# Two parts of the RWKV-7 time mixing reordered: triangle inverses by halves, and output products that wait for a run of like matmuls

## The chip, the cores and the metric

The kernel runs on one core of a Trainium2 chip. The metric is the device time of one execution in microseconds (us). The engines are named as the profile names them: PE is TensorE (matmuls), PEld its weight loads, DVE is VectorE, ACT is ScalarE, POOL is GpSimd, SP is SyncE, whose queue issues all DMAs here.

## The reference, cut to what matters

Two layers of a streaming encoder step. Each layer projects the normalised input, runs three groups of heads on the columns (a short convolution, a latent attention, and RWKV-7 time mixing), and projects their joined output back. The change is in the time mixing alone, which is this recurrence over 1104 tokens (64 of a running stream, 16 meta tokens, 1024 of a new stream) for 4 heads of width 64:

```python
def step(s, inp):
    r_t, w_t, k_t, v_t, kk_t, a_t = inp
    sa = jnp.einsum('bhvk,bhk->bhv', s, -kk_t)
    s = (s * w_t[:, :, None, :] + sa[..., None] * (kk_t * a_t)[:, :, None, :]
         + v_t[..., None] * k_t[:, :, None, :])
    return s, jnp.einsum('bhvk,bhk->bhv', s, r_t)
```

The kernel computes it in chunks of 64 tokens: inside a chunk the steps become products of 64 by 64 matrices and the inverse of a unit triangular matrix, and only the state goes from chunk to chunk.

## The kernel before, in words

A layer has three stretches. `inproj` and `inproj_rest` run the input projections: 24 matmuls of 128x384 (or 128x336) for each block of columns and each of three groups of tokens, in fp32r, an operand split into a high and a low half (`prj<-hhi,whi` and its two companions). Attention with half of the output projection follows, and then the rest of the output projection. PE is full of projections in the first stretch, and the time mixing is slipped in between them.

The time mixing of a layer has six parts, one for each pair of heads and group of six chunks (three groups for the first pair, then three for the second). Three generators work on them. `rwkv_prep` prepares a part. `rwkv_scan` carries the state through its six chunks (`xp` reads the state, `sp` writes the next one) and ends with the output products `yp`. `rwkv_finish` normalises them (DVE, ACT), transposes them on PE (`ym`) and gates them (POOL). A generator yields the tiles and PSUM pools it needs next. `pump`, called after each matmul, asks a model of the engines (`Meter`, with an assumed cost for each instruction) when these are ready, and runs a generator whose need is due; so the program's order is fixed when the kernel is built, by that model's times. The build then places the instructions of each engine, and each engine takes its own in order.

What `rwkv_prep` does, in the order of the steps that matter here:

- It loads the columns `lora` (a buffer of which there is one), passes their first half through three ACT steps (`sigmoid`) and one DVE step, and uses it in `ldp` and `icl`.
- `chunks(X1, ...)` makes the 64 by 64 matrices of the part, in 24 matmuls whose operands are 64 rows by 64 columns (`x<-wb,wx 64*64`).
- Their 16 by 16 diagonal blocks are summed out by DVE (`dg<-wq`), written to DRAM and read back with one block in each of 48 partitions (`tri`): two transfers in a row. There DVE inverts the 48 unit triangles in a loop over `n = 1 .. 14`, two instructions a step, a multiply into the scratch half `tm` and an add. A copy makes the transpose, and three transfers (one out, two in: `dg`, `dt`) bring both back, spread out by `wq<-dg,cst` and `wa<-dt,cst`.
- From the blocks' inverses the 64 by 64 inverses are put together by `inv` products, first 24 with `chunks(X2, ...)` (24 more `x`) behind them, then 48, then 24 with 48 `av` and `yv` products, then 24, and after these 48 `w`. All are matmuls of the 64*64 form.

A stretch of PE's order in which only such 64*64 matmuls stand is called a run here. `yp` is of the same form: 24 matmuls. In the kernel before, `rwkv_scan` issues them as soon as the state's last step is there (`yield uv, "rs"`). `prep` of part i+1 starts when the scan of part i has begun, and `scan` of part i+1 when its preparation is made, so a scan runs beside the next part's preparation.

Of the kernel before, what the change touches and what calls it, by code (L numbers as in the profile page):

```python
# [15 lines left out]
ALU = mybir.AluOpType  # L16
AX = mybir.AxisListType
# [14 lines left out]
GN = 384  # L32
# [4 lines left out]
BLK = 16  # L37
# [157 lines left out]
class Net:  # L195
# [729 lines left out]
    def rwkv_prep(self, l, i, g, hp):  # L925


        nc, I, O = self.nc, self.I, self.O
        tag = self.rwkv_tag(i)
        S = lambda s: self.S(tag, s)  # L930
        gc = slice(GN * g, GN * (g + 1))
        lora = self.small("lora", [128, 512])[:, :GN]
        nc.sync.dma_start(lora, self.zd[6, :, gc])
        wl = lora[0:64]
        self.sigmoid(wl, wl, 2.0)
# [2 lines left out]
        r, k, v = (wr[:, GN * x:GN * (x + 1)] for x in range(3))  # L938
# [23 lines left out]
        for t in range(3):  # L962
# [3 lines left out]
                                in0=ps[:, :GN].rearrange("p (t f) -> p t f", f=128),  # L966
                                in1=self.w0b[:, hc].unsqueeze(1).to_broadcast([128, 3, 128]), op=ALU.add)
# [16 lines left out]
        for t in range(3):  # L984
            tri = self.c(C_TRI0 if g == 0 and t == 0 else C_TRI, 128)
# [38 lines left out]
        def chunks(X, lhs, m, swap):  # L1024
            pj = [rp("x0"), rp("x1")]
            for t, c in quad:
                x = 1 - c if swap else c
                for j in range(2):
                    self.mm(pj[j][cr(x), 128 * t:128 * (t + 1)].rearrange("p (i n) -> p i n", i=2), lhs[cr(j), t, c, :],
                            arc(t, c, j), start=True, stop=True)  # L1030

            def masked(j):
                p3 = pj[j][:, :GN].rearrange("p (t n) -> p t n", t=3)
                nc.vector.tensor_tensor(out=X[:, j], in0=p3, in1=msk(m, 128), op=ALU.mult)
                if X is X1:
                    nc.scalar.activation(A[:, j], p3[:, :, 0:64], AF.Copy)
            return masked

        masked = chunks(X1, bk, C_X1, True)
        for j in range(2):  # L1040
            masked(j)
# [3 lines left out]
                                op=ALU.add, axis=AX.X)  # L1045
        scr = nc.dram_tensor(f"tri{l}_{g}_{hp}", (3, 6, 8, BLK, BLK), F32).ap()
        nc.sync.dma_start(scr[0].rearrange("t b r k -> (b r) t k"), dg)
        tri = self.small("tri", [128, 512])[:48].rearrange("p (i r k) -> p i r k", i=2, k=BLK)
        nc.sync.dma_start(tri[:, 0], scr[0].rearrange("t b r k -> (t b) r k"))
        yield kt, "rw"  # L1050
        for ts in ((0, 1, 2), (3, 4, 5)):
            o = turned(lambda t: wx[:, 128 * t:128 * (t + 1)], ts)
# [10 lines left out]
        o = turned(lambda t: v[:, 128 * t:128 * (t + 1)])  # L1063
# [2 lines left out]
        nc.scalar.activation(at, turned(lambda t: wb[:, GN * t:GN * t + 128]), AF.Copy)  # L1066

        up, tm = tri[:, 0], tri[:, 1]
        for n in range(1, BLK - 1):
            o = [48, n, BLK - 1 - n]  # L1070
            nc.vector.tensor_tensor(out=tm[:, :n, n + 1:], in0=up[:, :n, n:n + 1].to_broadcast(o), in1=up[:, n:n + 1, n + 1:].to_broadcast(o),
                            op=ALU.mult)
            nc.vector.tensor_tensor(out=up[:, :n, n + 1:], in0=up[:, :n, n + 1:], in1=tm[:, :n, n + 1:], op=ALU.add)
        nc.gpsimd.memset(tri[:, 0].rearrange("p r k -> p (r k)")[:, 0:BLK * BLK:BLK + 1], 1.0)
        nc.vector.tensor_copy(tm, up.rearrange("p r k -> p k r"))
        nc.sync.dma_start(scr[1:3].rearrange("x t b r k -> (t b) x r k"), tri)
        dq, dt = dg, self.small("dt", [128, 6, BLK])
# [10 lines left out]
        def prod(lhs, rhs, ps, cc=slice(0, 64)):  # L1088
            o = ps[:, :GN].rearrange("p (t n) -> p t n", n=64)
            for t in range(6):  # L1090
                for c in range(2):
                    self.mm(o[cr(c), t, cc], lhs[cr(c), t, :], rhs[cr(c), t, cc], start=True, stop=True)
            return o

        def block(dst, r, cc, o):
            rows = lambda c: slice(64 * c + r.start, 64 * c + r.stop)
            nc.scalar.activation(dst[rows(0), :, cc], o[rows(0), :, cc], AF.Copy)
            nc.vector.tensor_copy(dst[rows(1), :, cc], o[rows(1), :, cc])

        mk = lambda i: self.lev[:, i].unsqueeze(1).to_broadcast([128, 6, 64])  # L1100
        yield Q, Tm, kt, "rw+", "next"
        o = prod(A, Tm, self.psp("inv"))
        masked = chunks(X2, kt, C_X2, False)
        nc.scalar.activation(Pm, o, AF.Copy)
        yield Pm, "rw+"
        oq, ot = prod(Pm, Q, rp("inv")), prod(Q, Pm, rp("inv"))
        nc.vector.copy_predicated(Q, mk(0), oq)
        nc.vector.copy_predicated(Tm, mk(1), ot)
# [2 lines left out]

        lo, hi = slice(0, 32), slice(32, 64)
        yield Q, Tm, X2, uv, "rw+", "next"
        inv = prod(A, Tm, self.psp("inv"), lo)
        ps = [rp("av"), rp("yv")]
        o = [x[:, :GN].rearrange("p (j t n) -> p j t n", j=2, n=64) for x in ps]
# [6 lines left out]
        self.evict(AV, o[0])  # L1123
        self.evict(X2[:, :, :, 64:128], o[1])
        yield Pm, Q, "rw"
        block(Q, lo, hi, prod(Pm, Q, rp("inv"), hi))
        yield Q, AV, at, "rw+"

        ps = [rp("w"), rp("w")]
        o = lambda c, j, x: ps[c][cr(j), 192 * x:192 * (x + 1)].rearrange("p (t n) -> p t n", n=64)  # L1130
# [12 lines left out]
    def rwkv_scan(self, l, i, g, hp, dc, wb, kb, uv, wq, wx):  # L1143

        nc, I, O = self.nc, self.I, self.O
        rp = lambda s: self.ps(s, "rs")
        v4 = lambda x, n: x.rearrange("p (j t n) -> p j t n", j=2, n=n)
        X1, X2, QAV = v4(wq[:, 0:768], 128), v4(wx[:, 0:768], 128), v4(wq[:, 768:1152], 64)
        quad = [(t, c) for t in range(3) for c in range(2)]
        cr = lambda c: slice(64 * c, 64 * c + 64)  # L1150
        two = lambda x: x.rearrange("p (j n) -> p j n", j=2)
        if g == 0:
            nc.gpsimd.memset(X2[cr(1), :, 0, 0:64], 0.0)
        for t, c in quad:
            ci = 2 * t + c
            sample, meta = g == 0 and ci == 0, g == 0 and ci == 1
            b = cr(1 - c)
            if sample:
                s = self.state_tile()
                for j in range(2):  # L1160
                    nc.sync.dma_start(s[cr(j), cr(j)], I["wkv"][l, hp, cr(j), :])
            elif not meta:
                s = self.state
            if meta:
                nc.vector.tensor_copy(two(uv[b, ci, :]), QAV[b, :, t, :])
            else:
                yield s, "rs"
                sd = self.small("sd", [128, 128])
                nc.scalar.activation(sd, s, AF.Copy, scale=dc[:, ci:ci + 1])
                ps = rp("xp")  # L1170
                self.mm(ps[:, 0:128], wb[:, GN * t + 128 + 128 * c:GN * t + 256 + 128 * c], s, start=True, stop=True)
                nc.vector.tensor_tensor(out=two(uv[b, ci, :]), in0=two(ps[b, 0:128]), in1=QAV[b, :, t, :], op=ALU.add)
                nc.scalar.activation(X2[cr(c), :, t, 0:64], two(ps[cr(c), 0:128]), AF.Copy)
            yield uv[b, ci, :], "rs"
            ps = rp("sp")
            self.mm(ps[:, 0:128], kb[:, ci, :], uv[:, ci, :], start=True, stop=True)
            last = g == 2 and ci == 5
            dst = self.state_tile()
            for j in range(2):
                b = cr(j)  # L1180
                if meta:
                    nc.vector.tensor_scalar(dst[b, b], ps[b, b], dc[b, ci:ci + 1], None, op0=ALU.mult)
                else:
                    nc.vector.scalar_tensor_tensor(out=dst[b, b], in0=ps[b, b], scalar=dc[b, ci:ci + 1], in1=sd[b, b],
                                                   op0=ALU.mult, op1=ALU.add)
            if sample or last:
                for j in range(2):
                    nc.sync.dma_start(O["wkv"][l, 1 if sample else 0, hp, cr(j), :], dst[cr(j), cr(j)])
            self.state = dst
        nc.gpsimd.tensor_tensor(out=X2[:, :, :, 0:64], in0=X2[:, :, :, 0:64], in1=X2[:, :, :, 64:128], op=ALU.add)  # L1190
        yield uv, "rs"

        ps = rp("yp")
        for t in range(3):
            for j in range(2):
                for c in range(2):
                    b = cr(1 - c)
                    self.mm(ps[cr(c), 128 * t + 64 * j:128 * t + 64 * j + 64], X1[b, j, t, 64:128], uv[b, 2 * t + c, cr(j)],
                            start=True, stop=True)
        self.scanned = ps, wq, wx  # L1200
# [32 lines left out]
    def mix(self, main, side, streams, fill):  # L1233

        self.solo = self.prepped = self.projected = self.valued = self.queried = self.halved = False
        self.scored = self.steps = self.spent = 0
        streams = [[(), q] for q in streams]
        early = streams[ORDER.index("prepare")]
        self.side = [[(), q] for q in side] + [early]
        for _ in main:  # L1240
            pass
        self.projected, self.spent = True, NEVER
        self.side.remove(early)
        self.race(streams, fill)
        assert not self.side
# [292 lines left out]
```

## Time and profile before

| | |
|---|---|
| time, three runs | 1533.61, 1536.56 and 1537.31 us; median 1536.56 us |
| the profiled execution | 1536.26 us; span from the first to the last instruction 1534.3 us |
| PE, PEld | 1459.0 us busy (95%), 1306.4 us (85%) |
| DVE, ACT, POOL | 1063.0 us (69%), 769.3 us (50%), 258.0 us (17%) |
| granted TensorE clock | 0.989 of full speed, mean over the span |

PE's share says that only some 75 us of the span had no matmul in flight. These are spread over many waits of a few us or less, so the waits of PE, and what stands ahead of them on the other engines, are what to read. [...]

### The profile page before, as it was taken

The page shows a single profiled execution, that of the slowest core. Times are in us where ns is not written, and L with a number is a line of the kernel's source. Part 1 is how long each engine was busy: PE and PEld are TensorE (multiplying, and loading weights), DVE is VectorE, ACT ScalarE, POOL GpSimd, SP SyncE. Part 2 cuts the span into 40 slices and gives each one's busy share as a digit, 9 for nine tenths or more (in the row PEclk, how much of TensorE's full clock was granted, in tenths as well). Part 3 has the DMA queues.
Part 4 walks back from the last instruction along what each step waited for, and adds up shares of the span by engine and source line. Part 5 has one row for each costly group of instructions (what it writes and reads, how often), then busy time and mean ns, then how long its engine had stood idle before and what let it go on. Part 6 is the DMA issues. An engine that isn't in the chain of part 4 may idle for free.

```text
span 1534.3 us, 30679 instructions
## 1 busy us (share of the span) xinstructions
PE 1459.0 (95%) x12060; PEld 1306.4 (85%) x12060; DVE 1063.0 (69%) x2623; ACT 769.3 (50%) x1842; POOL 258.0 (17%) x281
## 2 busy tenths in 40 slices
PE   7999998999999999999999998899999999999996
PEld 7989887988887878779999888788988888778796
DVE  7566586766869676585845575876867787577666
ACT  7125454343668575563522354444456775555442
POOL 0212212221221101000011221312112211011002
PEclk9999999999999999999999999999999999999998
DMA  6332112322325101122423312122212341002123
GB/s 220 124 90 91 54 42 65 87 40 64 99 69 174 44 25 40 57 70 63 150 93 104 111 38 57 55 61 78 62 56 80 106 141 47 28 22 85 47 66 118
DMA packets 95327, 119.82 MB, mean 78 GB/s; under 512 B 41872, under 2 KB 74768, under 8 KB 95184
## 3 DMA queue, kind: packets, MB, share of 16 engines
q1 hardware_dynamic: 95184, 117.87, 25.0%
q8 instruction: 95, 1.56, 0.4%
q14 instruction: 48, 0.39, 0.1%
HBM read 81.24 MB, written 36.60 MB: 77 GB/s over the span
## 4 chain that ended last, share of the span: by engine, by line
PE 65%; DVE 17%; ACT 8%; issue 5%; DMA 3%; POOL 2%; SPq 0%; DVEq 0%; ACTq 0%; POOLq 0%
PE prj L81 33%; PE sc L81 6%; PE po L81 6%; PE tr L81 5%; DVE tri L81 3%; PE upq L81 3%; PE inv L81 3%; DVE wq L81 2%; PE val L81 1%; ACT wq L81 1%; DVE wlo L81 1%; DVE st L81 1%; PE upk L81 1%; PE tm L81 1%; PE w L81 1%
## 5 line engine op out<-in xcount | busy, mean ns | idle before, releaser
L81 PE MATMUL prj<-hhi,whi 128*128 128x384 f32 (+1 forms) x1152 | 391.3, 340 | 7.3 <-ACT hhi L81 6.4
L81 PE MATMUL prj<-hlo,whi 128*128 128x384 f32 (+1 forms) x1152 | 390.7, 339 | 0.6 <-DVE hlo L81 0.6
L81 PE MATMUL prj<-hhi,wlo 128*128 128x384 f32 (+1 forms) x1152 | 390.0, 339 | 0.8 <-DVE wlo L81 0.8
L81 PEld LDWEIGHTS prj<-hhi,whi 128*128 128x128 f32 x1152 | 218.6, 190 | 10.8 <-ACT hhi L81 6.4
L81 PEld LDWEIGHTS prj<-hlo,whi 128*128 128x128 f32 x1152 | 218.5, 190 | 4.9 <-DVE hlo L81 1.0
L81 PEld LDWEIGHTS prj<-hhi,wlo 128*128 128x128 f32 x1152 | 218.5, 190 | 3.8 <-DVE wlo L81 1.1
L81 PE MATMUL prj<-yhi,wo 128*128 128x384 f32 (+2 forms) x776 | 208.5, 338 | 2.1 <-DVE xn L81 2.0
L81 PE MATMUL sc<-ka,qa 128*128 128x264 f32 (+8 forms) x720 | 154.6, 335 | 3.9 <-ACT p L81 3.1
L81 ACT ACTIVATE p<-sc,st 128x144 f32<-128x144 f32 (+8 forms) x240 | 128.1, 542 | 42.8 <-DVE st L81 42.0
L81 PEld LDWEIGHTS prj<-yhi,wo 128*128 128x128 f32 x776 | 138.7, 188 | 5.1 <-DVE xn L81 3.7
L81 DVE TENSOR_REDUCE st<-sc 128x1 f32<-128x264 f32 (+8 forms) x240 | 117.7, 502 | 23.5 <-PE sc L81 21.8
L81 PE MATMUL prj<-ylo,wo 128*128 128x384 f32 (+2 forms) x388 | 130.2, 336 | 0.0
L81 ACT ACTIVATE pt<-tr 128x512 f32<-128x512 f32 (+3 forms) x172 | 90.6, 544 | 76.0 <-PE tr L81 74.5
L81 PEld LDWEIGHTS sc<-ka,qa 128*128 128x128 f32 (+1 forms) x720 | 112.2, 187 | 14.9 <-ACT p L81 8.2
L81 PE MATMUL tr<-cst,p 128*128 128x128 f32 (+2 forms) x752 | 115.4, 276 | 0.8 <-DVE st L81 0.2
L81 POOL TENSOR_TENSOR qa<-qt,qa 128x512 fp32r<-128x512 f32 (+1 forms) x40 | 49.0, 1228 | 337.9 <-ACT qa L81 337.9
L81 PEld LDWEIGHTS tr<-cst,p 128*128 128x128 f32 (+2 forms) x752 | 83.9, 140 | 23.6 <-issue 11.2
L81 PE MATMUL po<-pt,v 128*64 128x256 f32 (+3 forms) x864 | 94.3, 354 | 0.0
L81 ACT ACTIVATE whi<-wraw 128x1024 fp32r<-128x1024 f32 x48 | 50.7, 1056 | 81.8 <-PE prj L81 64.4
L81 DVE TENSOR_TENSOR tri<-tri 48x14 f32<-48x14 f32 (+6 forms) x336 | 84.1, 250 | 9.3 <-DMA tri<-tri 0.5
L81 DVE TENSOR_SCALAR p<-p,st 80x336 f32<-80x336 f32 (+5 forms) x144 | 80.9, 565 | 1.6
L81 DVE TENSOR_TENSOR wlo<-wraw,whi 128x1024 fp32r<-128x1024 f32 x48 | 67.8, 1412 | 12.7 <-ACT whi L81 12.2
(227 smaller groups left out, 2624.5 us busy)
## 6 DMA issues: line engine op xcount, KB each, us to landing
wraw<-w_in SPq DMA_DIRECT2D x48, 512.0 KB, 3.6
wraw<-w_out SPq DMA_DIRECT2D x32, 256.0 KB, 2.6
zd<-z SPq DMA_DIRECT2D x14, 576.0 KB, 3.3
wr<-zd SPq DMA_DIRECT2D x36, 192.0 KB, 2.9
gd<-gate SPq DMA_DIRECT2D x12, 552.0 KB, 3.2
yraw<-yd SPq DMA_DIRECT2D x8, 552.0 KB, 3.8
xn<-x SPq DMA_DIRECT2D x8, 552.0 KB, 4.0
xd<-xn SPq DMA_DIRECT2D x8, 552.0 KB, 2.7
```

The source lines that it names most:

```text
L81: r = f(*args, **kw)
```

## The change: what it does

Three things. The inversion runs on both 8 by 8 halves of a triangle at once, in 12 instructions, and puts the block between them in as two small matrix products, each a multiply over 8 x 8 x 8 elements and a sum over the last 8: 16 instructions in place of 28. Their scratch is the part's own `lora` buffer (`room`), which so stays in use until the inversion is done. The memset of the diagonal stands ahead of the loop in the code. And `self.bursts` counts the preparation's runs; the scan's `yp` waits until that count has risen (or no preparation is left).

```diff
-        lora = self.small("lora", [128, 512])[:, :GN]
+        room = self.small("lora", [128, 512])
+        lora = room[:, :GN]
...
+        self.bursts += 1
         masked = chunks(X1, bk, C_X1, True)
...
-        for n in range(1, BLK - 1):
-            o = [48, n, BLK - 1 - n]
-            nc.vector.tensor_tensor(out=tm[:, :n, n + 1:], in0=up[:, :n, n:n + 1].to_broadcast(o), in1=up[:, n:n + 1, n + 1:].to_broadcast(o),
-                            op=ALU.mult)
-            nc.vector.tensor_tensor(out=up[:, :n, n + 1:], in0=up[:, :n, n + 1:], in1=tm[:, :n, n + 1:], op=ALU.add)
-        nc.gpsimd.memset(tri[:, 0].rearrange("p r k -> p (r k)")[:, 0:BLK * BLK:BLK + 1], 1.0)
+        flat, room = tri.rearrange("p i r k -> p (i r k)"), room[:48]
+        nc.gpsimd.memset(flat[:, 0:BLK * BLK:BLK + 1], 1.0)
+        h = BLK // 2
+        two = flat[:, 0:2 * (h * BLK + h)].rearrange("p (b x) -> p b x", b=2)[:, :, 0:h * BLK].rearrange("p b (r k) -> p b r k", k=BLK)[:, :, :, 0:h]
+        for n in range(1, h - 1):
+            o = [48, 2, n, h - 1 - n]
+            part = room[:, 0:2 * n * (h - 1 - n)].rearrange("p (b r k) -> p b r k", b=2, r=n)
+            nc.vector.tensor_tensor(out=part, in0=two[:, :, :n, n:n + 1].to_broadcast(o), in1=two[:, :, n:n + 1, n + 1:].to_broadcast(o), op=ALU.mult)
+            nc.vector.tensor_tensor(out=two[:, :, :n, n + 1:], in0=two[:, :, :n, n + 1:], in1=part, op=ALU.add)
+        cube = room[:, 0:h * h * h].rearrange("p (i k j) -> p i k j", i=h, k=h)
+        between, mid = up[:, 0:h, h:], tm[:, 0:h, 0:h]
+        for x, y, o in ((between, up[:, h:, h:], mid), (up[:, 0:h, 0:h], mid, between)):
+            nc.vector.tensor_tensor(out=cube, in0=x.unsqueeze(2).to_broadcast([48, h, h, h]),
+                                    in1=y.rearrange("p j k -> p k j").unsqueeze(1).to_broadcast([48, h, h, h]), op=ALU.mult)
+            nc.vector.tensor_reduce(out=o, in_=cube, op=ALU.add, axis=AX.X)
...
         yield Q, Tm, kt, "rw+", "next"
+        self.bursts += 1
         o = prod(A, Tm, self.psp("inv"))
...
         yield uv, "rs"
+        n = self.bursts
+        yield (lambda: self.bursts > n or self.prepped,)
 
         ps = rp("yp")
```

The same line `self.bursts += 1` stands before the other runs of the preparation too (the 48 `inv`, the `inv` with `av` and `yv`, the last `inv`, the `w`). Because `Meter` plans by what it has seen issued, most of the program's order behind the first such place is new.

First place: DVE at the end of the third part's inversion in the first layer. `tri` is the triangles' tile; `kr` and `krt` belong to the attention's rotated keys; `wlo` is a weight tile's low half; `wr<-xp` and `state` are steps of the running scan. Before:

```order
L81 TENSOR_TENSOR tri_2219<-tri_2219 48x11x4
L81 TENSOR_TENSOR wlo_2408<-wraw_2321,whi_2407 128x1024
L81 TENSOR_TENSOR tri_2219<-tri_2219 48x12x3
L81 TENSOR_TENSOR wr_1419<-xp_2434,wq_1430 64x128
L81 TENSOR_TENSOR tri_2219<-tri_2219 48x12x3
L81 COPY u_2405<-par_79 128x2
L81 MEMSET u_2405 128x2
L81 TENSOR_TENSOR tri_2219<-tri_2219 48x13x2 x2
L81 TENSOR_TENSOR tri_2219<-tri_2219 48x14 x2
L81 COPY tri_2219<-tri_2219 48x256
L81 TENSOR_TENSOR wq_2069<-dg_2216,cst 128x6x64
L81 TENSOR_TENSOR wa_2068<-dt_2306,cst 128x384
```

And now, from just behind the copy of the triangles and one `kr` step:

```order
L81 SCALAR_TENSOR_TENSOR kr_2293<-krt_2294,rot 32x384
L81 TENSOR_TENSOR wlo_2382<-wraw_2291,whi_2381 128x1024
L81 SCALAR_TENSOR_TENSOR krt_2294<-krt_2294,rot 32x384
L81 TENSOR_TENSOR wr_1400<-xp_2413,wq_1411 64x128
L81 TENSOR_TENSOR kr_2293<-kr_2293,krt_2294 32x384
L81 COPY u_2379<-par_79 128x2
L81 MEMSET u_2379 128x2
L81 TENSOR_SCALAR lora_2707<-lora_2707 64x384
L81 TENSOR_TENSOR kr_2293<-kr_2293 32x384
L81 SCALAR_TENSOR_TENSOR state_128<-sp_2461,dc_1471,sd_2411 64x64 x2
L81 TENSOR_TENSOR wq_2042<-dg_2192,cst 128x6x64
L81 TENSOR_TENSOR wa_2041<-dt_2274,cst 128x384
```

Eleven rows that stood between the inversion's steps, or elsewhere, now stand between its copy and `wq<-dg`, the step of the next part's `lora` and a step of the scan's state among them.

Second place: PE at the second part's preparation in the first layer. `yp` of the first part stood alone between projections:

```order
L81 MATMUL prj_1767<-hlo_152,whi_1521 128x384
L81 MATMUL prj_1767<-hhi_144,wlo_1522 128x384
L81 MATMUL yp_1786<-wr_687,wq_828 64x64 x12
L81 MATMUL prj_1767<-hhi_145,whi_1521 128x384
L81 MATMUL prj_1767<-hlo_153,whi_1521 128x384
```

Now it stands between the last of the `x` and the 48 `inv` of the second part (a row of 12 is 24 matmuls in the profile):

```order
L81 MATMUL x_228_1823<-wb_1473,wx_1475 64x128
L81 MATMUL x_229_1824<-wb_1473,wx_1475 64x128
L81 MATMUL yp_1838<-wr_687,wq_828 64x64 x12
L81 MATMUL inv_1861<-wq_1411,wa_1410 64x64 x12
L81 MATMUL inv_1874<-wa_1410,wq_1411 64x64 x12
L81 MATMUL prj_1804<-hhi_140,wlo_1711 128x336
```

The five projections that stood between `x` and those `inv` products are gone from there, and the run around `yp` now reaches from the first `inv` to the last.

Third place: SP's queue around the third part's transfers in the first layer, before:

```order
L81 DMA lora_2757<-zd 128x384
L81 DMA wraw_2321<-w_in 128x1024
L81 DMA tri_2_0<-dg_2216 128x6x16
L81 DMA tri_2219<-tri_2_0 48x256
L81 DMA o_ckv<-ckv_1520 128x1104
L81 DMA kr_2323<-krc 32x256
L81 DMA o_kr<-kr_2323 32x1104
L81 DMA wraw_2411<-w_in 128x1024
L81 DMA tri_2_0<-tri_2219 48x2x256
L81 DMA dg_2216<-tri_2_0 128x6x16
```

and now:

```order
L81 DMA tri_2_0<-dg_2192 128x6x16
L81 DMA tri_2195<-tri_2_0 48x256
L81 DMA kr_2293<-krc 32x256
L81 DMA o_ckv<-ckv_1518 128x1104
L81 DMA lora_2707<-zd 128x384
L81 DMA wr_2713<-zd 128x384
L81 DMA tri_2_0<-tri_2195 48x2x256
L81 DMA wr_2713<-zd 128x384 x2
L81 DMA wraw_2385<-w_in 128x1024
L81 DMA dg_2192<-tri_2_0 128x6x16
```

The next part's `lora` load moved from ahead of both triangle transfers to just ahead of the one that writes the inverses out, and the `wr` loads came with it.

## Rows read from the trace of the kernel before

**Rows 1.** The page, part 1: busy us, share of the span, instructions.

```profile
PE 1459.0 (95%) x12060; PEld 1306.4 (85%) x12060; DVE 1063.0 (69%) x2623; ACT 769.3 (50%) x1842; POOL 258.0 (17%) x281
```

**Rows 2.** Waits of PE, whole span: total us, times, longest.

```profile
PE inv L81 <- DVE wa L81: 11.4, 3, 5.4
...
PE ym L81 <- DVE wq L81: 6.1, 3, 2.4
...
PE yp L81 <- DVE state L81: 3.7, 6, 1.1
```

**Rows 3.** Waits of PE from 830 to 1230 us (the second layer).

```profile
PE inv L81 <- DVE wa L81: 5.1, 1, 5.1
```

**Rows 4.** Timeline of PE: start, us, instruction, idle before and its releaser.

```profile
234.49 0.32 PE L81 MATMUL prj<-hlo,whi 128*128 128x336 f32 x1
240.17 1.43 PE L81 MATMUL inv<-wa 64*64 64x64 f32 x21 [5.36 <-DVE wa L81]
```

**Rows 5.** Timeline of DVE, the third part's inversion, first layer.

```profile
214.44 0.16 DVE L81 TENSOR_TENSOR tri<-tri 48x14 f32<-48x14 f32 x1
...
232.16 0.30 DVE L81 TENSOR_TENSOR wr<-xp,wq 64x128 f32<-64x128 f32 x1
...
234.29 0.37 DVE L81 COPY tri<-tri 48x256 f32<-48x256 f32 x1
238.77 0.56 DVE L81 TENSOR_TENSOR wq<-dg,cst 128x384 f32<-128x384 f32 x1 [4.10 <-DMA dg<-tri]
```

**Rows 6.** The page, part 5: one group (busy us, mean ns, idle before).

```profile
L81 DVE TENSOR_TENSOR tri<-tri 48x14 f32<-48x14 f32 (+6 forms) x336 | 84.1, 250 | 9.3 <-DMA tri<-tri 0.5
```

**Rows 7.** Windows, instructions on `tri` alone: stretch, length, DVE busy, POOL busy, clock, DMA.

```profile
214.40:234.30 19.90, 8.05 (x29) 0.00 (x0) 1.00 0.20 65
279.20:289.10 9.90, 5.38 (x29) 0.12 (x1) 1.00 0.20 59
```

**Rows 8.** Groups of instructions by form (busy us, mean ns).

```profile
L81 DVE TENSOR_TENSOR wo<-wraw,wo 128x512 fp32r<-128x512 f32 x32 | 21.9, 683 | 1.1
...
L81 DVE TENSOR_REDUCE gs<-wq 128x6 f32<-128x384 f32 x24 | 13.2, 550 | 4.6 <-ACT wq L81 4.0
...
L81 DVE TENSOR_REDUCE dg<-wq 128x96 f32<-128x384 f32 x12 | 9.7, 807 | 0.0
...
L81 DVE TENSOR_TENSOR tri<-tri 48x26 f32<-48x26 f32 x48 | 8.5, 177 | 1.4
```

**Rows 9.** Instructions on `lora`: ns min/median/max, first and last start; then its transfers.

```profile
L81 ACT ACTIVATE lora<-lora x36: 505/523/528, 53.5 to 1080.3; 64x384 f32<-64x384 f32 x36
...
L81 DVE TENSOR_SCALAR lora<-lora x12: 341/342/354, 55.1 to 1086.1; 64x384 f32<-64x384 f32 x12
...
DMA to landing us min/median/max: 2.3/2.4/6.0
```

**Rows 10.** Windows: stretch, length, PE, PEld, DVE, ACT, POOL busy, granted clock, DMA.

```profile
240.10:244.40 4.30, 4.23 (x56) 3.69 (x56) 2.92 (x7) 1.05 (x3) 0.00 (x0) 0.57 0.45 125
...
995.20:998.70 3.50, 3.41 (x52) 3.08 (x53) 2.25 (x6) 0.78 (x2) 0.00 (x0) 0.58 0.26 92
```

**Rows 11.** Timeline of PE around the first part's `yp`.

```profile
168.50 0.34 PE L81 MATMUL prj<-hhi,whi 128*128 128x384 f32 x1
...
168.85 0.34 PE L81 MATMUL prj<-hhi,wlo 128*128 128x384 f32 x1
169.12 0.91 PE L81 MATMUL yp<-wr,wq 64*64 64x64 f32 x24
...
170.25 0.34 PE L81 MATMUL prj<-hlo,whi 128*128 128x384 f32 x1
```

**Rows 12.** Timeline of PE, from `x` to the 48 `inv`, second part.

```profile
180.10 0.82 PE L81 MATMUL x<-wb,wx 64*64 64x128 f32 x22
...
182.49 0.92 PE L81 MATMUL inv<-wq,wa 64*64 64x64 f32 x24 [0.60 <-ACT whi L81]
183.21 0.90 PE L81 MATMUL inv<-wa,wq 64*64 64x64 f32 x24
```

More of the change, by code (lines that the diff above doesn't have):

```diff
@@ L1105, in rwkv_prep @@
         yield Pm, "rw+"
+        self.bursts += 1
         oq, ot = prod(Pm, Q, rp("inv")), prod(Q, Pm, rp("inv"))
@@ L1113, in rwkv_prep @@
         yield Q, Tm, X2, uv, "rw+", "next"
+        self.bursts += 1
         inv = prod(A, Tm, self.psp("inv"), lo)
@@ L1125, in rwkv_prep @@
         yield Pm, Q, "rw"
+        self.bursts += 1
         block(Q, lo, hi, prod(Pm, Q, rp("inv"), hi))
         yield Q, AV, at, "rw+"
+        self.bursts += 1
         ps = [rp("w"), rp("w")]
@@ L1235, in mix @@
         self.solo = self.prepped = self.projected = self.valued = self.queried = self.halved = False
-        self.scored = self.steps = self.spent = 0
+        self.scored = self.steps = self.spent = self.bursts = 0
         streams = [[(), q] for q in streams]
```

## The prediction, made before the changed kernel ran

> **What bounds the kernel now.** I read the page's busy line first: PE has a matmul in flight for 95% of the span [rows 1], so a faster DVE is worth nothing by itself, and the change can win or lose only where PE waits, where its clock is low, or where its matmuls follow one another badly. The waits of PE came second. Those the change touches are `inv` behind `wa` (11.4 us in three waits), `ym` behind the masks of `wq` (6.1 in three) and `yp` behind `state` (3.7 in six) [rows 2]; one wait of `inv` in the second layer is 5.1 [rows 3], and PE's timeline puts the 5.36 of the first layer at 234.8, where the third part's preparation ends a layer's projections and nothing is left to fill with [rows 4]. Third came DVE's timeline ahead of that wait: the inversion runs from 214.44 to 234.29, and then `wq<-dg` waits 4.10 for the way through DRAM [rows 5]. [...]
>
> The profiled execution took 1536.26 us (span 1534.3 and 2.0 around it), 0.3 below the median of 1536.56. The sum is made against 1536.3.
>
> **The inversion's price.** The group of 336 costs 84.1 us, 28 instructions or 7.0 us a part [rows 6]; alone it is 5.38, and 8.05 in the third part [rows 7]. The new form has 12 small instructions of 12 to 24 elements a partition. The 48x26 of before takes 177 ns, and the old group's mean, disturbed ones included, is 250: 2.1 to 3.0 us. Two multiplies over 512 elements go by the 128x512 row, 683 ns: 1.4. Two sums of 512 elements to 64 outputs were not seen; 384 elements to 6 outputs take 550 and to 96 outputs 807 [rows 8], some 2.9 ns for an output, so about 0.72 for 64, and 0.13 for 128 elements more: 0.85 each, 1.7. That is 5.2 to 6.1, and I take 5.8, a gain of 1.2 us a part; 8 halves of nested operands could bring it to no gain at all, an undisturbed run to 2.6. Over 12 parts DVE loses some 15 us of work. Nearly all of it lies beside matmuls and counts below only where PE waits.
>
> Alone, the 28 old instructions at [rows 8]'s prices are nearly as short as the new 16, so the number of instructions is not the whole price. [...]
>
> **The third part's wait, both layers.** DVE is full from 214.4 to 234.3: 8.05 on `tri` and nearly all the rest on other steps between. In the new order, 11 rows that stood among the inversion's steps now stand behind the copy, where DVE waited 4.10 anyway. I put the copy 4 to 5 us earlier: 1.2 to 2 by the price, the rest by the rows that moved. The way through DRAM stays, so `wa` comes 4 to 5 earlier and `inv` would lose most of its 5.4 and 5.1. What is late next is the scan: an `sp` that stands 22 projections ahead of that `inv`, some 22 x 0.175 = 3.9 us (0.175 is half of 168.50 to 168.85, two projections [rows 11]), needs `wr<-xp`, which DVE runs at 232.16 before [rows 5] and now only behind the copy and a `wlo`, and the scan's ACT step stands behind the three ACT steps of the next part's `lora`. I expect `sp` at 232.6 to 234 where PE, whose last projection ends at 234.8 [rows 4], wants it at 230.9, so part of the wait is not removed but moved. Of 5.4 and 5.1 I take back 3 each, 6 together (bounds 3 and 10).
>
> **The clock.** Behind these two waits PE ran 4.30 us at 0.57 and 3.50 at 0.58 [rows 10], which costs 4.30 x 0.43 + 3.50 x 0.42 = 3.3 us. With the wait halved I take half back: 1.5 (bounds 0 and 3.3).
>
> **The output products.** In the new order `yp` stands behind a run's start, the state long made, so its waits, 3.7 in six [rows 2], go, but for the layers' last: 3.5 (bounds 1 and 3.7). Then the form itself: alone, `yp` takes from 168.85 to 170.25, 1.40, of which two projections, one on either side, take 0.35 [rows 11]; 24 matmuls inside a run take 183.21 - 182.49 = 0.72 [rows 12]. So 1.40 - 0.35 = 1.05 stands against 0.72: 0.33 for each `yp` that no longer stands alone. There are seven of these: 2.3.
>
> Six `yp` now stand between `x` and the 48 `inv`, with no projection between. That saves a second change of form, 0.33 each, but the `inv` need what ACT and DVE make of `x`: from the last `x` at about 180.9 to the `inv` at 182.49 projections filled 1.6 us, and 0.60 was idle still [rows 12]. Now only a `yp` of 0.72 fills it. I charge 0.45 of new waiting each: 6 x (0.45 - 0.33) = +0.7. Unseen in this trace, so from both sides: -2 if the masks are always early, +6 if each waits a whole microsecond more.
>
> **The smaller waits of `inv` and `ym`.** The fifth part's `inv` waited 11.4 - 5.4 - 5.1 = 0.9 and gets 1.2 from the shorter inversion: -0.9. Most `ym` now come with more matmuls between `yp` and themselves; of 6.1 I take 1.5 back (bounds 0 and 5).
>
> **The held buffer.** `lora` has one buffer, free now only when the last sum is done. In nearly every part the next part's load, three ACT steps at 0.52 and DVE's 0.34 stand directly ahead of this part's `wq<-dg`. From the last sum: 2.4 to land, 1.57, 0.34 [rows 9]: 4.3, and the issue besides. The triangles' way: copy 0.37 and 4.10 of waiting [rows 5]: 4.5. They come almost together, so DVE would hold `wq<-dg` back by little, but ACT's steps take turns with evictions. I charge 0.2 in each of 10 parts, +2 (bounds 0 and 10, the upper where a landing is like the slowest, 6.0, and ACT is busy). On SP the load is now issued between the triangles' two transfers out and in, ahead of the one that writes the inverses; that is hidden, since the buffer frees before the copy that this transfer needs.
>
> **What the new order draws anew.** Three places were read closely; behind the first one, all is reordered, and the waits of 75 us without a matmul are drawn again. Planned waits that go come back elsewhere in part; I charge a third of the gains, +3.5 (bounds -3 and 10).
>
> **The sum.** -6 - 1.5 - 3.5 - 2.3 + 0.7 - 0.9 - 1.5 + 2 + 3.5 = -9.5. From 1536.3 that is 1526.8 us, and I say 1527.
>
> **The rivals.** *The wait only moves.* `sp` waits, behind `wr<-xp` and the `lora` steps on ACT, as long as `inv` did, the clock falls as before, and the merged runs wait. What speaks for it: the 11 rows put behind the copy. Against: `wr<-xp` has its place only a row or two later. Left are the 3.5 and 2.3 of `yp` less the 2 of the buffer and the 0.7 of the merged runs: 3.1, 1533. Chance 0.17.
>
> *The inversion is no shorter.* Nested operands of 8 by 8 by 8 with a stride of 16 run at 1.3 us an instruction and more, 2.1 + 4 x 1.3 = 7.3 a part against 7.0. Then the third part's wait gains only what the moved rows give, which the late scan takes again, and the newly drawn waits take 1.3 of the 3.1 that the rival before this keeps: 1534.5. For it: no row here has such operands in DVE. Against: the 48x26 of before is nested too and costs 177 ns. Chance 0.08.
>
> *The held buffer decides, and the kernel is slower.* Place: `lora`'s DVE step, directly ahead of `wq<-dg`. If it is ready later than the triangles by more than PE has in projections at that place, `wa` and `inv` wait. With a landing of 6.0 instead of 2.4 it is 4.3 + 3.6 - 4.5 = 3.4 late; of cover I know the 1.6 between `x` and `inv` worked out above, so that is the point from which it decides, and 1.8 a part is left. In 10 parts 18, in place of the forecast's 2: 1527 - 2 + 18 = 1543. For it: the order, and a single buffer. Against: the usual landing is 2.4, and `inv` waits for `wa` only three times in twelve parts. Chance 0.13.
>
> **How the numbers follow.** The forecast has 0.62, the rivals 0.17, 0.08 and 0.13. 0.3% of the time, 4.6 us, is about what a measurement of this kernel can tell from no change: faster is below 1532, slower above 1541. The forecast's own bounds, not all met at once, give 1516 to 1532. Of its 0.62, 0.59 lie below 1532, and 0.04 of the moved wait's: faster 0.63. The rest of these and the second rival make same, 0.03 + 0.13 + 0.08 = 0.24. Slower is the last: 0.13. The range of 8 in 10 goes from 1515, with some 0.06 below, to 1541, with the last rival's 0.1 above; the likeliest case alone is 1516 to 1532.
>
> **What would show it.** `tri` as 192 instructions, 16 a part, at 5.2 to 6.1 us a part, and `inv` behind `wa` under 3 us in all; a `sp` waiting for ACT or `wr` at the end of the projections says the wait moved. No `yp` behind `state` but the layers' last, and seven fewer changes of form. A granted clock above 0.57 in the stretch behind the third part. `wq<-dg` on DVE held behind `lora`, and `inv` waiting in more than three parts, would be the slower rival. My forecast is wrong if waits that this text does not name, at newly drawn places, exceed 7 us.

## The result, and the profile after

The changed kernel takes 1528.26 us (median of 6, 1526.55 to 1530.99) against 1536.71 for the kernel before beside it: a ratio of 0.9949, interval 0.9935 to 0.9962. The forecast was 1527 with 1516 to 1532 for its own case. A second measurement (below) gave 1529.78 and 0.9965, so the gain is some 5 to 8 us. The profiled execution took 1526.55 us, the lowest of the six and 9.7 below the profiled one of before, so the traces show some 1 us more gain than the medians. From its page:

```profile
span 1524.6 us, 30545 instructions
...
PE 1457.0 (96%) x12060; PEld 1305.6 (86%) x12060; DVE 1063.5 (70%) x2474; ACT 774.9 (51%) x1847; POOL 252.8 (17%) x281
```

DVE has 149 instructions fewer and is as busy as before [rows 1]. The span is 9.7 us shorter. Added up along PE's timeline to its last matmul, the time without a matmul went from 65.8 to 57.7 us, so 8.1 of the 9.7 are waits. PE's waits over the whole span (total, times, longest) show which:

```profile
PE sp L81 <- ACT wx L81: 9.1, 6, 3.7
PE inv L81 <- DVE wx L81: 6.4, 6, 1.4
...
PE tr L81 <- ACT pt L81: 5.4, 10, 1.1
PE tm L81 <- ACT wa L81: 4.2, 2, 2.1
...
PE xp L81 <- DVE state L81: 3.2, 5, 0.8
PE inv L81 <- DVE wa L81: 2.5, 2, 1.9
...
PE ym L81 <- DVE wq L81: 1.9, 2, 1.0
PE tr L81 <- DVE p L81: 1.7, 4, 0.4
PE w L81 <- DVE wq L81: 1.5, 2, 0.8
PE sc L81 <- POOL qa L81: 1.4, 2, 0.7
```

Against [rows 2]: `inv` behind `wa` fell from 11.4 to 2.5, `ym` from 6.1 to 1.9, and `yp` behind `state` (3.7) is gone. But `sp` behind ACT's `wx`, 0.2 before, is 9.1, and 3.65 of it stands in the third part of the first layer, 3.62 in the second. That is the wait that moved. PE's timeline there:

```profile
225.46 0.34 PE L81 MATMUL prj<-hhi,wlo 128*128 128x384 f32 x1
229.45 0.79 PE L81 MATMUL sp<-wr,wt 128*128 128x128 f32 x2 [3.65 <-ACT wx L81]
...
236.17 0.85 PE L81 MATMUL inv<-wa 64*64 64x64 f32 x21
```

`inv` no longer waits (5.36 in [rows 4]); `sp`, ahead of it, does. DVE's timeline shows why:

```profile
207.84 0.16 DVE L81 TENSOR_TENSOR lora<-tri 48x12 f32<-48x12 f32 x1 [0.15 <-DMA tri<-tri]
...
223.52 0.36 DVE L81 COPY tri<-tri 48x256 f32<-48x256 f32 x1
...
226.39 1.81 DVE L81 TENSOR_TENSOR wlo<-wraw,whi 128x1024 fp32r<-128x1024 f32 x1
228.23 0.55 DVE L81 SCALAR_TENSOR_TENSOR krt<-krt,rot 32x384 f32<-32x384 f32 x1
228.81 0.28 DVE L81 TENSOR_TENSOR wr<-xp,wq 64x128 f32<-64x128 f32 x1
...
232.76 0.64 DVE L81 TENSOR_TENSOR wq<-dg,cst 128x384 f32<-128x384 f32 x1
```

The copy is 10.8 us earlier than in [rows 5]. Of these, 6.6 are there when the inversion starts (207.84 in place of 214.44), and 4.2 are gained from its first step to the copy, 15.68 us in place of 19.85. `wr<-xp` is only 3.35 earlier, behind the copy now instead of ahead of it. ACT's `wx<-xp` starts at 229.13, after it, and `sp` follows. The inversion alone (stretch, length, DVE busy, POOL busy, clock, DMA), the third part and then an undisturbed one:

```profile
207.80:223.20 15.40, 5.93 (x16) 0.12 (x1) 1.00 0.09 38
271.50:279.00 7.50, 5.48 (x16) 0.12 (x1) 1.00 0.02 4
```

8.05 became 5.93, and 5.38 became 5.48 [rows 7]: undisturbed, the new form is no shorter at all. Its long instructions (busy us, mean ns):

```profile
L81 DVE TENSOR_TENSOR lora<-tri 48x512 f32<-48x512 f32 x24 | 26.7, 1113 | 1.5
...
L81 DVE TENSOR_REDUCE tri<-lora 48x64 f32<-48x512 f32 x24 | 16.2, 673 | 0.5
```

PE's runs of 64*64 matmuls fell from 79 to 68, and the first part's `yp` stands in the second part's run:

```profile
173.46 0.82 PE L81 MATMUL x<-wb,wx 64*64 64x128 f32 x22
174.06 0.86 PE L81 MATMUL yp<-wr,wq 64*64 64x64 f32 x24
175.98 0.92 PE L81 MATMUL inv<-wq,wa 64*64 64x64 f32 x24 [1.06 <-DVE wx L81]
```

The clock behind the third part's wait in the two layers (stretch, length, busy of PE, PEld, DVE, ACT, POOL, clock, DMA) is no better than in [rows 10]:

```profile
229.40:235.00 5.60, 5.55 (x18) 5.55 (x19) 4.36 (x9) 2.16 (x5) 3.22 (x3) 0.50 0.49 131
977.00:981.00 4.00, 3.96 (x13) 3.96 (x14) 3.89 (x9) 1.92 (x4) 3.24 (x3) 0.50 0.68 183
```

### The profile page after: what moved, and what is told of

Read it like the earlier page. It is cut to its first block, busy times and chain, and to the rows that moved or that the text cites. A ratio compares the mean times of both kernels' runs of the same rounds, so it can differ in the third digit from the quotient of the medians.

```text
span 1524.6 us, 30545 instructions
## 1 busy us (share of the span) xinstructions
PE 1457.0 (96%) x12060; PEld 1305.6 (86%) x12060; DVE 1063.5 (70%) x2474; ACT 774.9 (51%) x1847; POOL 252.8 (17%) x281
## 4 chain that ended last, share of the span: by engine, by line
PE 65%; DVE 17%; ACT 7%; issue 5%; DMA 4%; POOL 1%; SPq 0%; DVEq 0%; ACTq 0%; POOLq 0%
PE prj L81 34%; PE sc L81 6%; PE po L81 6%; PE tr L81 5%; PE inv L81 3%; PE upq L81 3%; DVE wq L81 2%; PE val L81 2%; DVE st L81 1%; DMA tri<-tri 1%; ACT p L81 1%; DVE lora L81 1%; DVE tri L81 1%; DVE p L81 1%; PE w L81 1%
## 5 line engine op out<-in xcount | busy, mean ns | idle before, releaser
L81 PE MATMUL prj<-yhi,wo 128*128 128x384 f32 (+2 forms) x776 | 204.5, 336 | 2.0 <-DVE xn L81 2.0
L81 PE MATMUL sc<-ka,qa 128*128 128x264 f32 (+9 forms) x720 | 156.9, 337 | 4.8 <-ACT p L81 2.1
L81 DVE TENSOR_REDUCE st<-sc 128x1 f32<-128x512 f32 (+9 forms) x240 | 118.3, 502 | 19.6 <-PE sc L81 18.2
L81 ACT ACTIVATE pt<-tr 128x512 f32<-128x512 f32 (+3 forms) x176 | 94.2, 550 | 66.2 <-PE tr L81 64.9
L81 DVE TENSOR_SCALAR p<-p,st 80x336 f32<-80x336 f32 (+5 forms) x144 | 84.5, 588 | 2.0
L81 PEld LDWEIGHTS po<-pt,v 128*64 128x64 f32 (+1 forms) x864 | 53.2, 136 | 27.1 <-issue 4.1
```

Of the source, the lines that this page charges most:

```text
L81: r = f(*args, **kw)
```

## The experiments

Each time is a median, each ratio is to the kernel before on the same chip, with its interval.

**Each part of the change alone.** In the first, the two lines `n = self.bursts` and the `yield` behind it go; in the second, the old loop stands in place of the new.

> The inversion by halves in the lora buffer, and the output products issued as before, without waiting for a run. Own theory: the two parts of the change pay about equally; alone the halves shorten the inversion by 1.1 us a part and move the third part's wait from inv to sp, with a gain of about 4 us: 1532 to 1533, the yp waits behind state (3.7 us) still there. Rival, all of the gain is the shorter inversion: 1528, as the full change. Rival, all of the gain is the place of the output products: 1536 to 1537.

> The old loop of 28 instructions, and the output products wait for the preparation's next run. Own theory: the yp waits behind state go (3.5 us), lone runs become fewer (2.3 us), and the 48 inv behind x and yp wait more (up to 6 us in six places), the third part's inv wait of 5 us a layer stays or is split: a gain of 2 to 5 us, 1532 to 1535. Rival, all from the place of the output products: 1528. Rival, all from the inversion: 1536 to 1537.

Halves alone: 1538.41, 1.0014 (1.0001 to 1.0026). Waiting alone: 1537.39, 1.0007 (0.9996 to 1.0019). Both own theories failed. Each time is near the rival that gave the whole gain to the other part, and these two rivals cannot both hold: alone neither part gains anything, and together they gain 5 to 8. In halves-alone the 48 `inv` of the third part wait 3.05 and 3.04 us on DVE in the two layers, in waiting-alone `inv` waits longer for `wa` than before:

```profile
PE inv L81 <- DVE wx L81: 6.6, 4, 3.0
```

```profile
PE inv L81 <- DVE wa L81: 13.4, 3, 6.5
```

Waits are not all of it. In the trace of halves-alone the time without a matmul, added up as above, is 62.5 us, 3.3 less than before, and what is gained there goes into the matmuls: PE is busy for 1462.2 us in place of 1459.0, with 84 runs of 64*64 matmuls in place of 79. Why was not traced further.

**The changed kernel again, the old loop in its order, and halves in the old order.** `Meter` plans by the instructions it is told. In the last two kernels one form is issued past it and the other is told to it but not issued, so that the order stays, but for some rows, while the inversion changes (shortened):

```
+        plan = Engine(nc, "vector", Unissued())      # told to Meter only
+        plan.tensor_tensor(...); plan.tensor_reduce(...)         # one form
+        nc.nc.vector.tensor_tensor(...)              # the other, issued past Meter
```

> The changed kernel once more, beside the next three on the same chip, so that differences of 4 us between its neighbours and the scratch-in-wa and scan-first kernels (1532) can be told from a difference of the chips. Own theory: 1528 and a ratio of 0.994 to 0.996 as before; those two kernels then are slower by added stretches at the half clock. Rival: about 1532 here too, the first measurement was on a kinder chip.

> The old loop of 28 instructions, while the planner is told the costs of the new 16, so that PE's order is that of the full change but for some 27 rows. It shows what the shorter inversion is worth in the new order. Own theory: DVE has 1.1 us a part more, in the third part 2, and sp there and inv in the fifth part wait that much longer, with the half clock behind: 4 to 7 us a kernel, 1532 to 1535. Rival, the planned order alone makes the gain: 1528. Rival, the inversion's length decides all: 1537.

> The inversion by halves, with its scratch in the part's wa tile, while the planner is told the old loop's costs and yp does not wait: PE's order is that of the kernel before but for two rows. It shows what the shorter inversion is worth in the old order. Own theory: as in the new order, where 16 instructions in place of 28 were worth 6 us (old loop in the new plan 1535.6, full change 1529.8): the third part's inv waits of 5.4 and 5.1 shrink by 2 to 3 us each, 1530 to 1532; then halves-alone at 1538 lost by the order that the planner drew from the shorter costs, and by the held buffer. Rival: in the old order DVE fills the freed time with other steps, and nothing is gained, 1535 to 1537; then the two parts of the change need one another.

The changed kernel: 1529.78, 0.9965 (0.9954 to 0.9977), a gain of 5.4 us, a little less than was expected. The old loop in the new order, beside it on the same chip: 1535.6, 1.0003 (0.9995 to 1.0012), 5.8 more. The inversion is not all that differs: the old loop has its scratch in `tm`, so `lora` comes free early, as in the scratch-in-`wa` kernel below (0.9974). By the two ratios the old loop costs 0.0029 of the time there, 4.5 us. So in the new order 16 instructions in place of 28 are worth 4.5 to 5.8 us, as expected. PE's waits with the old loop:

```profile
PE inv L81 <- DVE wa L81: 9.2, 4, 3.5
PE sp L81 <- ACT wx L81: 8.3, 6, 3.3
```

`inv` behind `wa` comes back to 9.2 from 1.9 in the changed kernel's trace beside it, beside an `sp` wait that stays; the time without a matmul goes from 58.3 to 64.1. Most of it is not the length of the steps. In the first layer's third part the old loop's steps take 7.84 us and the new ones, in the scratch-in-`wa` kernel, 5.93; but from the first step to the copy 26 other rows of DVE stand between the old steps and 17 between the new, and the copy comes after 23.39 us in place of 15.77. Fewer steps left fewer places for other work in between.

Halves in the old order: 1534.61, 0.9990 (0.9978 to 1.0002), less than expected, and no gain that can be told from none:

```profile
PE xp L81 <- DVE state L81: 13.0, 13, 2.7
...
PE inv L81 <- DVE wa L81: 1.5, 2, 0.8
```

The 11.4 of [rows 2] went almost wholly, to 1.5, and `xp`, which stands next in PE's order, waits 13.0 for the scan's state in place of 7.6. The same 16 instructions are worth 1.6 us at the median, which is not clear of nothing, in the order where the scan is late behind them, and 4.5 to 5.8 in the new one.

**The buffer.** In one kernel the scratch lies in idle columns of `wa` instead of `lora`; in the other the old loop of the kernel before uses `lora` as scratch.

```diff
-        flat, room = tri.rearrange("p i r k -> p (i r k)"), room[:48]
+        flat, room = tri.rearrange("p i r k -> p (i r k)"), wa[:48, GN:GN + 512]
```

> The full change, but the inversion's scratch lies in 512 columns of the part's wa tile that hold nothing then, so lora comes free early, as before the change. PE's order is the same. Own theory: the held buffer puts the lora and wr loads ahead of the transfer that writes the inverses out, which then takes 4.5 us to the next transfer's issue in the third part in place of 1.9, and puts lora's DVE step ahead of wq<-dg. Freed, the fifth part's inv waits (0.6 and 1.9) go, the third part's inverses come 2 to 3 us earlier, where inv has 2.3 us to spare already and sp waits for something else: a gain of 2 to 3 us on the full change, about 1526. Rival, the held buffer costs nothing: 1528, within 1 us. Rival, it is what holds the third part: 1520 or less.

> The kernel before with its old loop, but the loop's scratch in the lora buffer, which so stays in use until the inversion is done. PE's order is the one of before. Own theory: the load, three ACT steps and DVE's step now come behind the inversion, ahead of wq<-dg; in the third part, where inv waits for wa already, that adds up to 2 us a layer: 1538 to 1541. Rival, the hold is free: 1536 to 1537. Rival, the hold is what made the full change good, by taking loads out of the projections' way: 1532 or less.

Hold alone: 1537.95, 1.0019 (1.0009 to 1.0028), a loss of some 3 us, as large as was expected, but mostly not where: in the third part `inv` waits 5.80 and 5.90 in place of 5.36 and 5.06, while `ym` behind `wq` went from 6.1 to 8.7 and `yp` behind `state` from 3.7 to 5.8. Freed in the new order: 1532.48, 0.9974 (0.9964 to 0.9984). That is no gain; the expected 2 to 3 us did not come. The clock in the trace of it is 0.985, where the changed kernel's traces have 0.990 and 0.988. `sp` waits as long as in the changed kernel, and the fifth part's `inv` in the second layer longer, 3.3:

```profile
PE sp L81 <- ACT wx L81: 9.1, 6, 3.6
...
PE inv L81 <- DVE wa L81: 3.3, 1, 3.3
```

**The scan first.**

```diff
+                with self.tc.high_priority():
-                nc.vector.tensor_tensor(out=two(uv[b, ci, :]), in0=two(ps[b, 0:128]), ...
+                    nc.vector.tensor_tensor(out=two(uv[b, ci, :]), in0=two(ps[b, 0:128]), ...
```

> The full change, but the scan's DVE step that reads xp (wr<-xp) has priority over other work of DVE. PE's order is nearly the same. Own theory: the 3.65 us wait of sp for wx<-xp in the third part of each layer is held by that step's late place (228.81, behind the copy, a wlo and three kr); put ahead of the copy it lets sp run without a wait, and inv then waits for wa, some 3 us in place of none: a gain of 0.5 to 2 us a layer with the clock, 1525 to 1527. Rival, the sp wait is worth its length and the half clock behind it, 6 us a layer: 1516 to 1518. Rival, ACT's three lora steps hold wx, not DVE: no change, 1528.

1531.94, 0.9976 (0.9965 to 0.9988): not faster than the changed kernel. The waits:

```profile
PE inv L81 <- DVE wa L81: 10.3, 4, 3.3
...
PE sp L81 <- ACT wx L81: 2.7, 5, 0.9
```

With `wr<-xp` ahead of the copy, `sp` hardly waits, so it was DVE's step that held ACT and PE, not the `lora` steps. But `inv` then waits for `wa` instead: 9.1 + 2.5 became 2.7 + 10.3. It is one wait with two names, and DVE's queue between 208 and 234 is what it is made of.

**Another run for `yp`.** The count in front of the first `inv` and the `x` goes.

```diff
         yield Q, Tm, kt, "rw+", "next"
-        self.bursts += 1
         o = prod(A, Tm, self.psp("inv"))
```

> The full change, but the run of the first 24 inv and the x is not counted, so that yp joins the next one, the 48 inv, and projections stand between x and those inv again. Own theory: the waits of inv behind yp (6.4 us in six places) go, some 0.33 us for each of six more changes of form comes: a gain of 3 to 4 us on the full change, 1524 to 1525. Rival, the order behind is drawn again and waits of the same size come at other places: 1528 to 1533.

1521.35, 0.9913 (0.9898 to 0.9927): 8.4 us under the changed kernel beside it, more than twice what was expected, and for another reason:

```profile
PE inv L81 <- DVE wa L81: 7.2, 6, 1.4
PE inv L81 <- DVE wx L81: 6.0, 6, 1.4
...
PE sp L81 <- ACT wx L81: 1.6, 5, 0.5
```

The waits behind `wx`, which were to go, are 6.0 instead of 6.4. The two PSUM banks that the 48 `inv` need are those of `x`, which DVE's masks (`wx<-x`) free, and two projections beside `yp` don't cover that: in the first layer's second part 0.70 is left. What went, against the changed kernel's trace beside it, is the `sp` wait (9.1 to 1.6), with 5.3 more of `inv` behind `wa` in its place, and the waits of `tr` for `pt` in the attention behind (5.2 to 0.4, while `po` now waits 1.1 for `pt`). The time without a matmul is 52.4 us in place of 58.3. The rest is likely the clock: this trace is of the slowest of the six runs (1525.13, clock 0.989), the other five had 0.991 to 0.995, and the twelve runs of the changed kernel 0.985 to 0.991. Why the order behind came out better was not traced.

> The later-run kernel (1521.4) with the inversion's scratch in wa, so that lora comes free early; PE's order is the same. Own theory: as between the full change and its scratch-in-wa form (1529.8 and 1532.5), freeing the buffer brings nothing here: 1520 to 1524. Rival, the held buffer costs what the old loop showed (2.8 us): 1518 to 1519.

> The old loop of 28 instructions, and yp waiting for the run of the 48 inv, as in the later-run kernel. Own theory: the better place of yp pays without the halves too, but less, since the third part's wait of inv stays: 1530 to 1533. Rival, the place of yp alone is worth the whole 14 us of the later-run kernel: 1521 to 1524. Rival, it brings nothing without the halves, as the waiting alone did (1537): 1535 to 1538.

With the scratch in `wa` as well: 1518.90, 0.9891 (0.9868 to 0.9913), the fastest kernel here, below the expected 1520 to 1524 and in the range of the rival that the held buffer has its price here too. But there are four runs, and the interval overlaps that of the kernel before it, so what the free buffer gives is not settled. `inv` behind `wa` is 3.3 there in place of 7.2:

```profile
PE inv L81 <- DVE wx L81: 5.6, 6, 1.3
...
PE inv L81 <- DVE wa L81: 3.3, 4, 1.4
```

With the old loop and the same place for `yp`: 1543.05, 1.0050 (1.0031 to 1.0070), slower than before and than any expectation. `sp` and `inv` both wait:

```profile
PE inv L81 <- DVE wa L81: 9.1, 3, 6.7
...
PE sp L81 <- ACT wx L81: 5.2, 2, 4.7
```

## Why the prediction was right, point by point

The time was right to 1.3 us, and the likeliest case came: most of the old waits went, and part of one moved. That it is so near is luck in part, since several terms were off, in both directions, and made up for one another.

- *The inversion's price*: forecast 5.8 us a part, measured 70.4 / 12 = 5.9. Its parts were off: the multiply over 512 took 1.11 and not 0.68, the sum 0.67 and not 0.85 (its 0.13 for 128 elements more agrees with [rows 8]: (683 - 177) / (512 - 26) = 1.04 ns an element, as an estimate). Of the two the multiply is the slow step. And the gain of 1.2 a part holds only beside other work: undisturbed it is 5.48 against 5.38.
- *The third part's wait*: forecast as partly moved from `inv` to `sp`, and it was, at the place and behind the step that was named. Kept are 5.4 + 5.1 - 3.65 - 3.62 = 3.2, at the low bound, not 6. From the inversion's first step the copy came 4.2 earlier, as forecast (4 to 5). What failed is where the two engines would meet: `sp` started at 229.45, earlier than the forecast's 232.6 to 234, but PE, all of which ran earlier, was ready for it at 225.80 and not at 230.9. That ACT's `lora` steps take part in it was wrong: with DVE's step first, `sp` hardly waited.
- *The clock*: forecast 1.5 back, and more was lost: 5.60 us at 0.50 and 4.00 at 0.50 cost 4.8, where 4.30 at 0.57 and 3.50 at 0.58 cost 3.3. The half clock came behind the moved wait as it had behind the old one. The sign that the prediction names, a clock above 0.57 there, did not come.
- *The output products*: `yp` behind `state` went wholly, 3.7 for 3.5. There are 11 runs fewer, not 7; what that gave was not measured by itself, but PE is busy for 2.0 us less in all. The merged runs wait about as forecast: `inv` behind `wx` is 6.4 in six places where the trace of before had 4.2 in four. The cover behind `x` was misread on the way: the 0.60 of waiting is part of the 1.6 us up to the `inv` [rows 12], so projections filled 1.0 of it.
- *The smaller waits*: `ym` gave 4.2 and not 1.5; the fifth part's `inv` gave nothing back (0.6 and 1.9 are left).
- *The held buffer*: forecast +2. It costs some 3 in the old order; freed in the new one nothing came back that could be measured. Not settled.
- *What the new order draws anew*: forecast +3.5. `inv`, `sp`, `yp`, `ym` and the merged runs account for 8.9 - 8.9 + 3.7 + 4.2 - 2.2 = 5.7 of the 8.1 us of waits; the other 2.4 are what redrawn waits gave on balance. The term had the wrong sign, inside its bounds, and this and `ym` made up for the third part and the clock.

By the last of its own signs the prediction fails. It calls itself wrong if waits that it does not name exceed 7 us at new places, and four kinds that the list of before does not have add up to 5.4 + 1.7 + 1.5 + 1.4 = 10.0: the attention's `tr` behind `pt` and `p`, `w` behind `wq` and `sc` behind `qa`. The time held because other unnamed waits shrank as much, above all these two, to 3.2 and 4.2 (from the trace of before, with the `sp` wait as it was):

```profile
PE xp L81 <- DVE state L81: 7.6, 11, 1.6
PE tm L81 <- ACT wa L81: 6.8, 4, 3.4
...
PE sp L81 <- ACT wx L81: 0.2, 1, 0.2
```

What the forecast did not see is that its terms cannot be added up part by part. Alone, halves lose some 2 us, and the waiting brings no difference that can be told; in the new order the halves are worth 4.5 to 5.8, in the old one no more than can be told from nothing. That is shown. Why the planner's order is good with both together was not traced step by step; that a like edit with a later run gains 14 us with the halves and loses 7 without says that no part has a price of its own.

## What to carry to other kernels

Where PE is 95% busy and a queue of another engine is full for 20 us, a shorter step in it or a priority may only rename the wait, as here: `inv` behind `wa` and `sp` behind `wx` were 11.4 + 0.2 before, 2.5 + 9.1 with shorter steps and 10.3 + 2.7 with the priority; in the later-run kernel with the scratch in `wa` both were short, 3.3 + 1.7. So ask what PE wants next behind the wait that goes. Where a planner draws the order from assumed costs, measure a cost and an order apart, by telling the planner one thing and issuing another; here they did not add, as the halves gave 1.6 in one order and 4.5 to 5.8 in the other. And try a second place before settling on one: one line's difference in the count was worth as much as the whole change.

## What the runs showed of the hardware

The same instructions behind the same waits came with a clock of 1.00 and with one of 0.55. In the changed kernel and in its form with the scratch in `wa`, PE's order is the same; from the start of a wait of 0.72 for `qa` in the second layer's attention on, these are two stretches of 3 us in each (columns as above), of the changed kernel and then of the other:

```profile
1203.00:1206.00 3.00, 1.94 (x15) 1.43 (x14) 3.00 (x10) 2.27 (x9) 0.70 (x1) 1.00 0.26 80
1206.00:1209.00 3.00, 2.44 (x21) 2.14 (x23) 2.96 (x11) 3.00 (x13) 0.51 (x1) 1.00 0.27 71
```

```profile
1210.00:1213.00 3.00, 1.79 (x15) 1.37 (x14) 3.00 (x9) 2.30 (x10) 0.76 (x1) 1.00 0.29 94
1213.00:1216.00 3.00, 2.67 (x12) 2.49 (x13) 2.70 (x10) 2.49 (x11) 0.13 (x1) 0.55 0.26 71
```

In the second kernel the clock is 0.55 behind it, and 12 matmuls fall into the 3 us in which the other has 21. The wait of `tr` that follows is 0.59 there and 0.64 in the changed kernel, so longer waits are not the reason. Two traces of the changed kernel itself differ in the same way: at this place of the first layer the 3 us up to 457.90 in one and up to 458.80 in the other have 15 matmuls each and 1.26 and 1.28 us without one, and the 3 us behind them a clock of 1.00 and of 0.64. In the changed kernel's second measurement the three fastest of twelve runs (1525.57 to 1527.18 us) have a mean clock of 0.989 to 0.991, the three slowest (1531.96 to 1532.71) 0.985 to 0.987. As an estimate, 0.004 of 1528 us is 6 us, so such stretches would make most of that difference, and a single trace shows one draw of them.

A copy of 48x256 on DVE took 0.37 in [rows 5], and 2.28 in the first part of each layer now, where it starts while POOL is in a `zd<-z` product and ends with it; in the first layer:

```profile
110.26 2.28 DVE L81 COPY tri<-tri 48x256 f32<-48x256 f32 x1
```

```profile
108.68 3.62 POOL L81 TENSOR_TENSOR zd<-z 128x1151 f32<-128x1151 f32 x1 [6.20 <-issue]
```

The two end together, 110.26 + 2.28 = 112.54 against 108.68 + 3.62 = 112.30. What held the copy is not shown: `wlo<-wraw,whi` on DVE, begun at 109.13 beside the same product, took 1.20, where the median of its 48 is 1.22.

Nor is this a price of the change alone. In the kernel before, the copy came after that product, but a step of the inversion met it, and took 2.16 us where the step of the same size ahead of it took 0.19; it ends at 111.61, the product at 111.55:

```profile
109.45 2.16 DVE L81 TENSOR_TENSOR tri<-tri 48x50 f32<-48x50 f32 x1
```

```profile
109.44 2.11 POOL L81 TENSOR_TENSOR zd<-z 128x1151 f32<-128x1151 f32 x1 [6.57 <-DVE tri L81]
```
